# One encoder layer on one core: loads of a head's q and k apart from their rounding, first factors of w_down kept in raw buffers, weights rounded three blocks ahead

## The chip, the cores and the metric

The program runs on 1 core of one Trainium2 chip. The metric is the device time in microseconds (us) of one execution. A core has a matrix engine (PE, with its own weight loads PEld), a vector engine (DVE), a scalar engine (ACT), GpSimd (POOL), a sync engine (SP) whose work here is to issue DMAs, and 16 DMA engines that all queues share. Each engine runs its own instructions in the order written in its program; across engines they wait on semaphores.

## What is computed

Shortened from the reference, batch 1, 512 tokens, width 2048, 8 heads of 128, feed-forward width 5632, all float32:

```python
h = rms_norm(x, pre_mix_g)
z = h @ w_in                       # [q | k | v | u], 1024 columns each
a = chunked_attention(q, k, v, rel_bias)      # chunks of 64, own and 8 before
p = multiscale_pool(u, pool_w, pool_scale)    # trailing means of 2, 4, 8, 16 tokens, minus u
x = x + rms_norm(concat(a, p) @ w_o, post_mix_g)
h = rms_norm(x, pre_ffn_g)
up = causal_dwconv(h @ w_up)
y = (gelu(up[:F]) * up[F:]) @ w_down
out = x + rms_norm(y, post_ffn_g)
```

## The kernel before

**Arithmetic.** A float32 product is made of two rounded parts: `split` writes the rounded operand `hi` on ACT and the rest `lo` on DVE, and `mm3` issues three matmuls. Tile names end in `h` and `l` for these parts and in `r` for the raw load. The large projections use seven products of halves instead of eight (`mm2`, `pairs.order`), with sums and differences of weights made on DVE.

**Order.** PE's instructions stand in the order written in the program. Those of the other engines are put into each engine's queue by a scheduler that works with its own estimate of times; `tc.issue_after(x)` holds an instruction behind another. Buffers are rings by tag: `raw` has 5 tiles of 128x1024 and holds raw weights on their way in, `w4` has 8 and holds their rounded parts (4 pairs), `hT` holds the activations. A new tile of a ring waits until whatever used its place is done, a store to DRAM included.

**Weights.** `Weights` holds one list of blocks (`specs`) in order of use. `get` takes the next and loads and rounds up to `ahead` blocks beyond it. The load is issued on SP's queue, the rounding goes to ACT and DVE.

**The mixing part**, which takes the first 600 us or so, runs in these stages:

1. Head 0's q and k, straight from the input (to about 30 us); then `v_steps(0)`: the first half of v, 16 steps of 12 matmuls, while DVE, ACT and POOL make the sums and differences of the input (`x_sums`). `v_spill(0)` stores that half to DRAM (`vd`).
2. q and k of heads 1 to 7 (`qk_product`, to about 223 us), 2.8 us a product. Each head's result is stored to `zqk`. The list `more_sums` advances one step at a time: copies and adding copies of blocks of w_o and w_down from DRAM to DRAM on POOL's queue, each paced by a small instruction on DVE and POOL (`pace`).
3. `v_steps(1)`: the second half of v (blocks 4 to 7, then 0 to 3), interleaved with the attention of heads 0 to 2. `scores(h)` multiplies q with k and issues the softmax on DVE and ACT; `turn(h)` transposes the probabilities on PE and rounds them into `pth`, `ptl`; `values(h)` multiplies them with v. `load_head(h)` loads the bias and `zqk` of a head, scales (`zq` times `RR`) and rounds them (`qkh`, `qkl`); `v_load` loads v and rounds it (`vh`, `vl`). Both are called as one piece: `load_head(h + 1)` at the end of `scores(h)`.
4. `u0` to `u7` (`project`), each two weight blocks and 48 matmuls, interleaved with the attention of heads 3 to 7 and the pooling (`pool_keep`, `pool_mix`). `pool_mix` writes through one buffer `mx` and stores to `pooled`.
5. w_o (`wo_product`), from about 440 us.

Three of the first factors of w_down that are used much later (`READY`, six halves) are rounded in advance in this part and stored as rounded parts to DRAM (`rw01`, `rw11`, `rw02`, with `h` and `l`): three halves among the blocks of `v_steps(0)`, three among those of `v_steps(1)`, their parts in `w4` tiles (`keep_ready` issues the two stores).

Of the kernel before, what the change touches and what calls it, by code (L numbers as in the profile page):

```python
# [15 lines left out]
P = 128  # L16
# [63 lines left out]
def encoder_layer(ctx: ExitStack, tc: tile.TileContext, x, xT, vecs, rel, post_mix, post_ffn,  # L80
# [175 lines left out]

    READY_AT = {0: (2, 4, 6), 1: (3, 5, 7)}
    ready_parts = [(at, j) for at in READY for j in range(2)]
    READY_OF = {0: ready_parts[:3], 1: ready_parts[3:]}

    def v_and_ready_specs(g):
        specs = []
        for n, spec in enumerate(v_specs(g)):
            specs.append(spec)
            if n in READY_AT[g]:
                (cc, i), j = READY_OF[g][READY_AT[g].index(n)]
                specs.append((f"rw{cc}{i}_{j}", first_block(cc, i - 1, 0)[:, 2 * j:2 * j + 2, :], 2, 512))
        return specs

    def keep_ready(g, n):  # L270
        if n not in READY_AT[g]:
            return
        (cc, i), j = READY_OF[g][READY_AT[g].index(n)]
        for dest, v in zip(ready_w[cc, i], weights.get(f"rw{cc}{i}_{j}")):
            nc.sync.dma_start(dest[:, 2 * j:2 * j + 2, :], f32(v))
# [4 lines left out]
    for g in range(4):  # L280
        specs += u_specs(2 * g)
        if g:
            specs += pm_spec(g - 1)
        specs += u_specs(2 * g + 1)
    for i in WO:
        for cc in range(2):
            specs += wo_specs(i, cc)
        if i == 1:
            specs += pm_spec(3)
# [4 lines left out]

    weights = Weights(specs, load_w, 4)
    weights.limit = FIRST_PART
# [87 lines left out]
    def v_steps(i, ps):  # L384
        for n, c in enumerate(VORDER[i]):
            w = weights.get(f"v{i}_{c}", 2 if (i, n) == (1, 0) else None)
            if not i:
                pairs.prefetch(4 - FIRST_PART + weights.used)
            for j in range(2):
                kb = 2 * c + j  # L390
                for t in range(NT):
                    mm3(ps[t], g_tokens(hT, kb, t), part(w, j), n == j == 0, n == 7 and j == 1)
                if j:
                    keep_ready(i, n)
                    if not i:
                        pairs.prefetch(4 - FIRST_PART + weights.used)
                yield

    def v_spill(i, ps):
        for p in range(2):  # L400
            v = raw4(f"vs{p}").rearrange("p (a b) -> p a b", a=2)
            for t in range(2):
                nc.scalar.activation(v[:, t], ps[2 * p + t], AF.Copy)  # L403
            nc.sync.dma_start(vd[i][:, 2 * p:2 * p + 2, :], v)
# [35 lines left out]
    class Pairs:  # L440
# [12 lines left out]
        def load(self, k, i):  # L453
            def raw(what, tile_, m, kh):
                load_w.last = nc.sync.dma_start(tile_, w_qk[k + 1, m, kh]).ins
                self.raw[k, what] = tile_

            if i == 1:
                raw("x", p0.tile([P, 1024], F32, tag="wx", bufs=3, name="wx"), 0, 0)
                raw("w", raw4("ww"), 1, 0)  # L460
            elif i == 2:
                raw("z", raw4("wz"), 0, 1)
            elif i == 5:
                raw("y", raw4("wy"), 1, 1)

# [48 lines left out]
    psr = bank("R")  # L514
    token_sums(psr, ssum)
    rstd(rt, psr[:, :NT])
    v_spill(0, psv)

# [35 lines left out]
    def qk_keep(k, i):  # L554
# [18 lines left out]
        elif i == 4:  # L573
            one, m, a = qk_z.pop((k, "1")), qk_z.pop((k, "m")), qk_banks.pop((k, "a"))
            z = p0.tile([P, 2, S], F32, tag="z", bufs=2, name="z")
            nc.vector.tensor_add(z[:, 0, :T], one[:, 0, 0], one[:, 0, 1])
# [13 lines left out]
    for k, i in [at for at in pairs.order if at[0] is not None]:  # L590
# [24 lines left out]
    with tc.tile_pool(name="p1", bufs=2, reuse_waits="tile") as p1:  # L615
# [34 lines left out]

        def load_head(h):
            state["bias", h] = t512("bias", bufs=1)
            nc.sync.dma_start(state["bias", h], rel[h])
            nc.vector.memset(state["bias", h][:CHUNK, S - CHUNK:], -1e30)
            v = p1.tile([P, 2, S], F32, tag="zq", bufs=1, name="zq")
            nc.sync.dma_start(v, zqk[h])
            nc.vector.tensor_mul(v, v, RR)
            pair = [p1.tile([P, 2, S], F32R, tag="qk" + p, bufs=1, name="qk" + p) for p in "hl"]
            split(*pair, v)
            state["qk", h] = [tuple(p[:, n, :] for p in pair) for n in range(2)]  # L660

        def v_load(i):
            vh, vl = (acc8(f"v{p}{i}", "B", F32R).rearrange("p (a b) -> p a b", a=NT) for p in "hl")
            nc.sync.dma_start(f32(vl), vd[i])
            for t in range(NT):
                split(vh[:, t, :], vl[:, t, :], f32(vl)[:, t, :], rt[:, t:t + 1])
            state["v"] = vh, vl

        def scores(h):
            (q, k), bias = state.pop(("qk", h)), state.pop(("bias", h))  # L670
            products = [bank(f"s{h}_{t}") for t in range(1, NT)]
            products = [products[0][:, 256:], *products]
# [17 lines left out]
            if h + 1 < HEADS:  # L690
                load_head(h + 1)

# [62 lines left out]

        load_head(0)
        v_load(0)
        for h in range(3):
            run(3 if not h else 1)
            scores(h)  # L760
# [4 lines left out]
            more_sums(1)  # L765
            run(2)
            turn(h)
        run(1)
        v_spill(1, psv)

        def mid(h):
            def step():
                values(h)
                more_sums(1)
                if h == 2:
                    scores(3)
                if h == 3:
                    v_load(1)
            return step

        for j in range(8):
            ps = project(f"u{j}", mid(2 if j == 0 else j + 1) if j not in (1, 7) else None)
            if 1 <= j <= 5:
# [918 lines left out]
```

## Time and profile before

| | us |
|---|---|
| three runs: median (lowest, highest) | 1928.85 (1921.6, 1929.78) |
| the profiled execution, its time | 1925.9 |
| its span, first to last instruction | 1924.1 |
| PE busy | 1873.8 (97%) |
| DVE busy | 1541.6 (80%) |
| ACT busy | 1082.5 (56%) |
| POOL busy | 302.3 (16%) |

How to read it: the span is PE's program almost from end to end, so what can be won is where PE stands still, and where it runs at a lower granted clock. "Idle before, releaser" in a view names what ended a wait. Times in views count from the span's start. A wait for several semaphores is put down to the one that came last. Busy time of engines other than PE costs nothing by itself; it counts where PE waits for it.

### The profile page before, as it was taken

To read this page: it belongs to the slowest core of one execution; us is meant where nothing else is said; L and a number is where in the kernel's file an instruction comes from. 1 tells how busy PE (TensorE), PEld (TensorE's weight loads), DVE (VectorE), ACT (ScalarE), POOL (GpSimd) and SP (SyncE) were. 2 spreads that over 40 slices of the span, in tenths; PEclk is the share of its full clock that TensorE was granted. 3 is DMA by queue.
4 is the path that set the end of the run, shared out by engine and by line. 5 is a ranking of instruction groups with operands and counts; after the bars stand their busy time and mean duration, and the time that the engine had idled before them with its cause. 6 is when DMAs were issued, how large, how long until landed. Compare 5 with 4: busy or idle time off the path is not lost.

```text
span 1924.1 us, 25433 instructions
## 1 busy us (share of the span) xinstructions
PE 1873.8 (97%) x9598; PEld 1593.8 (83%) x9598; DVE 1541.6 (80%) x1800; ACT 1082.5 (56%) x1376; POOL 302.3 (16%) x398
## 2 busy tenths in 40 slices
PE   9999869999999999999999999999999999999998
PEld 7788757877888888888888888888888888888886
DVE  6988565867768898878888888888887799898875
ACT  8545434535646566656565656656565665565553
POOL 3211110111000022121212121222211001101101
PEclk9999979999999999999999999999999999999999
DMA  8579897789887488888888988898988977876785
GB/s 279 185 247 284 250 301 240 208 223 305 297 251 288 134 215 199 199 201 199 208 204 196 209 200 201 201 197 196 207 191 269 350 230 174 198 197 170 172 234 146
DMA packets 139770, 426.01 MB, mean 221 GB/s; under 512 B 11968, under 2 KB 15424, under 8 KB 133952
## 3 DMA queue, kind: packets, MB, share of 16 engines
q0 software_dynamic: 54864, 173.56, 44.9%
q1 hardware_dynamic: 84784, 250.84, 37.5%
q8 instruction: 75, 1.23, 0.2%
q14 instruction: 47, 0.39, 0.1%
HBM read 370.35 MB, written 104.33 MB: 247 GB/s over the span
## 4 chain that ended last, share of the span: by engine, by line
PE 86%; DVE 5%; DMA 5%; ACT 2%; issue 1%; SPq 0%; POOL 0%; DVEq 0%; POOLq 0%; ACTq 0%
PE qa L164 18%; PE qa L170 9%; PE qg L164 9%; PE qg L170 5%; PE qd L164 4%; PE pa L156 4%; PE pa L158 4%; PE pa L159 4%; PE qd L170 2%; PE m L158 2%; PE m L156 2%; PE m L159 2%; PE pg L156 2%; PE pg L158 2%; PE pg L159 2%; DMA zq<-zqk 1%
## 5 line engine op out<-in xcount | busy, mean ns | idle before, releaser
L164 PE MATMUL qa<-gT,wfh 128*128 128x512 f32 x1152 | 290.7, 394 | 4.5 <-ACT vs L403 3.5
L138 ACT ACTIVATE wfh<-wx 128x1024 fp32r<-128x1024 f32 x192 | 203.5, 1060 | 156.8 <-PE qg L164 59.2
L139 DVE TENSOR_TENSOR wfl<-wx,wfh 128x1024 fp32r<-128x1024 f32 x192 | 234.7, 1222 | 64.7 <-ACT wfh L138 47.4
L164 PEld LDWEIGHTS qa<-gT,wfh 128*128 128x128 f32 x1152 | 207.9, 189 | 42.7 <-ACT vs L403 3.7
L1319 POOL DMA_DIRECT2D wx<-in_w_up x122 | 104.6, 857 | 506.2 <-DVE wfl L139 478.0
L138 ACT ACTIVATE wfh<-wy 128x1024 fp32r<-128x1024 f32 x96 | 101.9, 1061 | 117.3 <-PE qg L164 64.1
L164 PE MATMUL qg<-h,wfh 128*128 128x512 f32 x656 | 165.7, 394 | 0.0
L170 PE MATMUL qa<-gT,wfl 128*128 128x256 f32 x1152 | 160.8, 282 | 0.0
L170 PEld LDWEIGHTS qa<-gT,wfl 128*128 128x128 f32 x1152 | 151.2, 190 | 4.6
L164 PEld LDWEIGHTS qg<-h,wfh 128*128 128x128 f32 x656 | 122.9, 188 | 28.0
L139 DVE TENSOR_TENSOR bl<-b,bh 128x2048 fp32r<-128x2048 f32 x56 | 127.3, 2286 | 22.8 <-ACT bh L138 11.7
L138 ACT ACTIVATE bh<-b 128x2048 fp32r<-128x2048 f32 x56 | 105.8, 1911 | 47.2 <-DVE b L1077 20.2
L139 DVE TENSOR_TENSOR wfl<-wy,wfh 128x1024 fp32r<-128x1024 f32 x96 | 117.2, 1221 | 16.1 <-ACT wfh L138 9.3
L156 PE MATMUL pa<-bh,ah 128*128 128x512 f32 x320 | 126.1, 394 | 0.0
L158 PE MATMUL pa<-bl,ah 128*128 128x512 f32 x320 | 125.8, 393 | 0.0
L159 PE MATMUL pa<-bh,al 128*128 128x512 f32 x320 | 125.5, 392 | 0.0
L139 DVE TENSOR_TENSOR wfl<-wz,wfh 128x1024 fp32r<-128x1024 f32 x48 | 58.7, 1223 | 54.2 <-PE qa L164 54.1
L164 PE MATMUL qd<-gT,wfh 128*128 128x512 f32 x384 | 95.7, 391 | 0.0
L170 PEld LDWEIGHTS qg<-h,wfl 128*128 128x128 f32 x656 | 89.4, 188 | 7.5
L170 PE MATMUL qg<-h,wfl 128*128 128x256 f32 x656 | 91.6, 282 | 0.0
L164 PEld LDWEIGHTS qd<-gT,wfh 128*128 128x128 f32 x384 | 72.0, 188 | 16.2
L164 PE MATMUL qa<-h,wfh 128*128 128x512 f32 x328 | 83.2, 395 | 0.0
(551 smaller groups left out, 4386.6 us busy)
## 6 DMA issues: line engine op xcount, KB each, us to landing
wx<-in_w_up POOLq DMA_DIRECT2D x122, 512.0 KB, 5.9
b<-in_w_down SPq DMA_DIRECT2D x32, 1024.0 KB, 6.7
wt<-in_w_o POOLq DMA_DIRECT2D x24, 1024.0 KB, 12.6
wx<-in_w_up SPq DMA_DIRECT2D x43, 512.0 KB, 5.4
wz<-in_w_up SPq DMA_DIRECT2D x41, 512.0 KB, 5.6
wy<-in_w_up SPq DMA_DIRECT2D x41, 512.0 KB, 4.6
wy<-in_w_up POOLq DMA_DIRECT2D x41, 512.0 KB, 6.7
sum<-part POOLq DMA_DIRECT2D x38, 512.0 KB, 5.9
```

The lines of the kernel that those rows point to most:

```text
L138: rounded = nc.scalar.activation(hi, src, AF.Copy)
L139: rest = nc.vector.tensor_sub(lo, src, f32(hi))
L156: nc.tensor.matmul(ps, l[0], r[0], start=first, stop=False, skip_group_check=onto)
L158: nc.tensor.matmul(low, l[0], r[1], start=False, stop=False, skip_group_check=onto)
L159: nc.tensor.matmul(ps, l[1], r[0], start=False, stop=last, skip_group_check=onto)
L164: nc.tensor.matmul(ps, w[0][:, kb], pairs[kb][0], start=fresh and not kb, stop=last, skip_group_check=not fresh)
L170: nc.tensor.matmul(ps[:, sl], w[1][:, kb], pair[:, sl], start=False, stop=last, skip_group_check=not fresh)
L1319: nc.gpsimd.dma_start(self.raw[k, what], self.block(k, m, kh), accum_op=ALU.add)
```

## The change

It touches the mixing part alone.

- `load_head` becomes three: `load_bias` (the load alone), `load_z` (the load of `zqk` alone) and `ready_head` (scaling, rounding, and the load of the next head's `zq` right behind). The scaling waits behind the instruction that `split` last gave to DVE (`tc.issue_after(split.rest)`). The memset in the bias moves into `scores`, ahead of its use. `ready_head(h + 1)` is called two steps of v after `scores(h)` in stage 3, and inside or behind a `project` in stage 4.
- `v_load` keeps the load, `v_ready` rounds, behind `turn(0)` (and behind `u2` for the second half).
- All six halves of `READY` move into stage 4, one behind each of `u0` to `u5`; their rounded parts lie in two of the five tiles of the ring `raw` instead of `w4`.
- `Weights` runs 3 blocks ahead, not 4, until `weights.ahead = 4` behind `u7`.
- `v_spill(0)` stands ahead of `rstd` and writes through a `z` tile (pool `p0`, 2 tiles) instead of `raw`; one `wx` and one `wy` load change places between `raw` and `p0`.
- `more_sums` takes two steps fewer in stage 2 (at product 3 of heads 6 and 7) and two more in stage 4.

```diff
     def load_w(name, src, a, b):
         n = a * b
-        raw, hi, lo = raw4(name + "r"), w4(name + "h"), w4(name + "l")
+        raw = raw4(name + "r")
+        if name[:2] == "rw":
+            hi, lo = (big.tile([P, 1024], F32R, tag="raw", bufs=5, name=name + p) for p in "hl")
+        else:
+            hi, lo = w4(name + "h"), w4(name + "l")
...
-    READY_AT = {0: (2, 4, 6), 1: (3, 5, 7)}
+    READY_AT = {0: (), 1: ()}
...
-    READY_OF = {0: ready_parts[:3], 1: ready_parts[3:]}
+    READY_OF = {0: (), 1: ready_parts}
+    READY_U = {j: j for j in range(6)}
...
-    weights = Weights(specs, load_w, 4)
+    weights = Weights(specs, load_w, 3)
...
-            v = raw4(f"vs{p}").rearrange("p (a b) -> p a b", a=2)
+            v = raw4(f"vs{p}").rearrange("p (a b) -> p a b", a=2) if i else z_tile()
...
+    v_spill(0, psv)
     rstd(rt, psr[:, :NT])
-    v_spill(0, psv)
...
-        if i in (3, 7, 4) and (k, i) != (0, 3):
+        if i in ((3, 7, 4) if 0 < k < 5 else (7, 4)):
             more_sums(1)
...
-        def load_head(h):
+        def load_bias(h):
             state["bias", h] = t512("bias", bufs=1)
             nc.sync.dma_start(state["bias", h], rel[h])
-            nc.vector.memset(state["bias", h][:CHUNK, S - CHUNK:], -1e30)
-            v = p1.tile([P, 2, S], F32, tag="zq", bufs=1, name="zq")
-            nc.sync.dma_start(v, zqk[h])
-            nc.vector.tensor_mul(v, v, RR)
+
+        def load_z(h):
+            state["z", h] = p1.tile([P, 2, S], F32, tag="zq", bufs=1, name="zq")
+            nc.sync.dma_start(state["z", h], zqk[h])
+
+        def ready_head(h):
+            v = state.pop(("z", h))
+            with tc.issue_after(split.rest):
+                nc.vector.tensor_mul(v, v, RR)
             pair = [p1.tile([P, 2, S], F32R, tag="qk" + p, bufs=1, name="qk" + p) for p in "hl"]
             split(*pair, v)
             state["qk", h] = [tuple(p[:, n, :] for p in pair) for n in range(2)]
+            if h + 1 < HEADS:
+                load_z(h + 1)
...
         def scores(h):
             (q, k), bias = state.pop(("qk", h)), state.pop(("bias", h))
+            with tc.issue_after(split.rest):
+                nc.vector.memset(bias[:CHUNK, S - CHUNK:], -1e30)
...
-        load_head(0)
+        load_z(0)
+        load_bias(0)
         v_load(0)
         for h in range(3):
-            run(3 if not h else 1)
+            if not h:
+                run(2)
+                ready_head(0)
+            run(1)
             scores(h)
             more_sums(1)
             run(1)
             if h:
                 values(h - 1)
             more_sums(1)
-            run(2)
+            run(1)
+            ready_head(h + 1)
+            run(1)
             turn(h)
+            if not h:
+                v_ready()
...
+            if j in READY_U:
+                keep_ready(1, j)
             if j < 7:
                 pool_keep(j // 2, j % 2, ps)
-                more_sums(2 if j == 6 else 1)
+                more_sums(1 + j % 2)
         u7 = ps
         more_sums.paced = False
+        weights.ahead = 4
```

PE's own instructions keep their order. On the other engines the order moves; two places matter below. The first is DVE's queue where stage 2 passes into stage 3. Before, with `v_6` and `v_7` the weight blocks of v that PE takes next, `gT` the activations that are put back, `zm` and `pth` parts of heads 7 and 0:

```order
L636 CAST pth<-tmp 128x128
L636 CAST ptl<-tmp 128x128
L654 MEMSET bias 64x64
L657 TENSOR_TENSOR zq<-zq,RR 128x1024
L142 SCALAR_TENSOR_TENSOR gT_131<-xr_2005,vec,gT_131 128x256
L139 TENSOR_TENSOR v_6l<-v_6r,v_6h 128x1024
L572 TENSOR_TENSOR zm<-zb,zm 128x512
L142 SCALAR_TENSOR_TENSOR gT_131<-xr_2005,vec,gT_131 128x256 x3
```

The same place with the change:

```order
L139 TENSOR_TENSOR v_6l<-v_6r,v_6h 128x1024
L588 TENSOR_TENSOR zm<-zb,zm 128x512
L142 SCALAR_TENSOR_TENSOR gT_131<-xr_1973,vec,gT_131 128x256 x3
L142 SCALAR_TENSOR_TENSOR gT_132<-xr_1983,vec,gT_132 128x256 x3
L139 TENSOR_TENSOR v_7l<-v_7r,v_7h 128x1024
L142 SCALAR_TENSOR_TENSOR gT_132<-xr_1983,vec,gT_132 128x256
L320 MEMSET pace 128x1
L139 TENSOR_TENSOR v_0l<-v_0r,v_0h 128x1024
L593 TENSOR_TENSOR z<-zm 128x512
L595 TENSOR_TENSOR z<-qa_1735,z 128x256
L320 MEMSET pace 128x1
L678 TENSOR_TENSOR zq<-zq,RR 128x1024
```

The memset in the bias and the scaling of head 0 stood ahead of `v_6l`; now the scaling stands behind `v_6l`, `v_7l` and `v_0l`, and the memset behind the rounding of the head.

The second is ACT's queue around the first softmax (`s,sm<-s,nm` is the exponential of one of its four tiles, `pth` the probabilities turned by PE). Before:

```order
L138 ACTIVATE v_1h<-v_1r 128x1024
L138 ACTIVATE qkh<-zq 128x1024
L685 ACTIVATE s,sm<-s,nm 128x128
L138 ACTIVATE rw_0h<-rw_0r 128x1024
L141 ACTIVATE vh_2136<-vl_2137,rt 128x512 x4
L685 ACTIVATE s,sm<-s,nm 128x256
L138 ACTIVATE v_2h<-v_2r 128x1024
L685 ACTIVATE s,sm<-s,nm 128x384
L685 ACTIVATE s,sm<-s,nm 128x512
```

With the change:

```order
L138 ACTIVATE v_1h<-v_1r 128x1024
L714 ACTIVATE s,sm<-s,nm 128x128
L714 ACTIVATE s,sm<-s,nm 128x256
L138 ACTIVATE v_2h<-v_2r 128x1024
L714 ACTIVATE s,sm<-s,nm 128x384
L138 ACTIVATE rw_0h<-rw_0r 128x1024
L714 ACTIVATE s,sm<-s,nm 128x512
L138 ACTIVATE qkh<-zq 128x1024
```

The four roundings of v and those of the next head left the middle of the softmax; one rounding of a w_down factor (`rw_0h`) still stands ahead of its last exponential.

More of the change, by code (lines that the diff above doesn't have):

```diff
@@ L265, in v_and_ready_specs @@
             if n in READY_AT[g]:
-                (cc, i), j = READY_OF[g][READY_AT[g].index(n)]
-                specs.append((f"rw{cc}{i}_{j}", first_block(cc, i - 1, 0)[:, 2 * j:2 * j + 2, :], 2, 512))
+                specs.append(ready_spec(*READY_OF[g][READY_AT[g].index(n)]))
         return specs
     def keep_ready(g, n):
-        if n not in READY_AT[g]:
+        at = READY_U if g else {m: k for k, m in enumerate(READY_AT[0])}
+        if n not in at:
             return
-        (cc, i), j = READY_OF[g][READY_AT[g].index(n)]
+        (cc, i), j = READY_OF[g][at[n]]
         for dest, v in zip(ready_w[cc, i], weights.get(f"rw{cc}{i}_{j}")):
@@ L387, in v_steps @@
             if not i:
-                pairs.prefetch(4 - FIRST_PART + weights.used)
+                pairs.prefetch(3 - FIRST_PART + weights.used)
             for j in range(2):
@@ L392, in v_steps @@
                     mm3(ps[t], g_tokens(hT, kb, t), part(w, j), n == j == 0, n == 7 and j == 1)
-                if j:
+                if j and not i:
                     keep_ready(i, n)
-                    if not i:
-                        pairs.prefetch(4 - FIRST_PART + weights.used)
+                    pairs.prefetch(3 - FIRST_PART + weights.used)
                 yield
@@ L458, in load @@
             if i == 1:
-                raw("x", p0.tile([P, 1024], F32, tag="wx", bufs=3, name="wx"), 0, 0)
+                raw("x", raw4("wx") if not k else p0.tile([P, 1024], F32, tag="wx", bufs=3, name="wx"), 0, 0)
                 raw("w", raw4("ww"), 1, 0)
@@ L463, in load @@
             elif i == 5:
-                raw("y", raw4("wy"), 1, 1)
+                raw("y", raw4("wy") if k else p0.tile([P, 1024], F32, tag="wx", bufs=3, name="wy"), 1, 1)
         def make(self, k, i):
@@ L515, in encoder_layer, with z_tile @@
     token_sums(psr, ssum)
+    def z_tile():
+        return p0.tile([P, 2, S], F32, tag="z", bufs=2, name="z")
+    v_spill(0, psv)
     rstd(rt, psr[:, :NT])
-    v_spill(0, psv)
     def spread1():
@@ L664, in v_load, with v_ready @@
             nc.sync.dma_start(f32(vl), vd[i])
+            state["v"] = vh, vl
+        def v_ready():
+            vh, vl = state["v"]
             for t in range(NT):
-                split(vh[:, t, :], vl[:, t, :], f32(vl)[:, t, :], rt[:, t:t + 1])
-            state["v"] = vh, vl
+                with tc.issue_after(split.last):
+                    split(vh[:, t, :], vl[:, t, :], f32(vl)[:, t, :], rt[:, t:t + 1])
         def scores(h):
             (q, k), bias = state.pop(("qk", h)), state.pop(("bias", h))
+            with tc.issue_after(split.rest):
+                nc.vector.memset(bias[:CHUNK, S - CHUNK:], -1e30)
             products = [bank(f"s{h}_{t}") for t in range(1, NT)]
```

17 lines of the change are left out of this document (15 added, 2 removed).

## Prediction

> **What bounds the kernel now.** I read the page's totals first, then who waited for whom on PE, then PE's, DVE's and ACT's timelines where those waits lie.
>
> ```profile
> PE 1873.8 (97%) x9598; PEld 1593.8 (83%) x9598; DVE 1541.6 (80%) x1800; ACT 1082.5 (56%) x1376; POOL 302.3 (16%) x398
> PE   9999869999999999999999999999999999999998
> PEclk9999979999999999999999999999999999999999
> ```
>
> PE sets the end. The 41 us in which it stands still lie almost wholly in slices 5 and 6 and a few places beside them, all in the mixing part. PE's own list of waits says for whom:
>
> ```profile
> PE pt L699 <- DVE s L688: 17.6, 6, 5.2
> PE v L158 <- DVE v_6l L139: 6.4, 1, 6.4
> PE s L156 <- DVE ptl L139: 3.9, 1, 3.9
> PE qa L164 <- ACT vs L403: 3.5, 1, 3.5
> PE s L158 <- DVE qkl L139: 2.5, 1, 2.5
> PE m L156 <- ACT wo_3h L138: 2.4, 1, 2.4
> PE m L158 <- DVE wo_3l L139: 1.6, 1, 1.6
> PE qa L164 <- ACT wfh L138: 1.1, 1, 1.1
> ```
>
> The first column of numbers is the total in us. After a long wait the matmuls themselves are slow; the windows show it as granted clock (PEclk), PE busy being the second number:
>
> ```profile
> 235.00:240.00 5.00, 4.13 (x10) 3.26 (x11) 5.00 (x10) 1.59 (x3) 0.00 (x0) 0.50 0.31 105
> 240.00:245.00 5.00, 2.50 (x12) 1.94 (x11) 3.55 (x7) 0.00 (x0) 1.23 (x4) 0.84 0.81 225
> 245.00:250.00 5.00, 5.00 (x18) 4.08 (x17) 1.22 (x1) 2.01 (x2) 0.00 (x0) 0.72 1.00 342
> 270.00:275.00 5.00, 4.77 (x15) 4.10 (x16) 1.20 (x2) 2.19 (x4) 0.00 (x0) 0.50 1.08 296
> 295.00:300.00 5.00, 2.55 (x7) 2.26 (x8) 4.66 (x10) 0.77 (x3) 0.00 (x0) 0.55 0.85 154
> 300.00:305.00 5.00, 5.00 (x19) 4.04 (x18) 3.47 (x12) 2.91 (x5) 1.25 (x4) 0.76 0.48 141
> 395.00:400.00 5.00, 5.00 (x19) 4.30 (x19) 4.95 (x12) 2.76 (x6) 1.57 (x4) 0.71 0.75 230
> 465.00:470.00 5.00, 4.37 (x11) 3.46 (x12) 4.20 (x5) 2.75 (x3) 1.16 (x1) 0.54 1.06 323
> ```
>
> I charge a window with its PE busy time times (1 - PEclk): 2.1 + 0.4 + 1.4 = 3.9 us from 235 to 250, 2.4 at 270, 1.1 + 1.2 = 2.3 from 295 to 305, 1.5 at 395, 2.0 at 465.
>
> **The change, part by part.** PE's instructions and their order stay, so the sum runs over its waits, in six places.
>
> A, end of the first half of v (74 to 91 us).
>
> ```profile
> 74.56 2.11 PE L164 MATMUL qa<-gT,wfh 128*128 128x512 f32 x8 [1.06 <-ACT wfh L138]
> 87.12 3.63 PE L164 MATMUL qa<-gT,wfh 128*128 128x512 f32 x8 [3.46 <-ACT vs L403]
> 86.47 1.09 ACT L403 ACTIVATE vs<-v 128x512 f32<-128x512 f32 x2 [1.66 <-DVE wy L481]
> 59.97 2.32 DVE L139 TENSOR_TENSOR rw_0l<-rw_0r,rw_0h 128x1024 fp32r<-128x1024 f32 x1
> ```
>
> PE loses 1.06 + 3.46 us and 1.5 more to the clock (3.63 against 2.11 for the same eight matmuls): 6.0. The copies `vs` of v waited for a `raw` buffer until DVE had added `wy`. With the change they go to a `z` tile and DVE has three subtractions less before this point (2.32 us the quoted one). I count 5.5 us won. Bounds: 0, if DVE stays late for another reason, to 6.0.
>
> B, first head (229 to 250 us).
>
> ```profile
> 228.17 0.11 DVE L654 MEMSET bias<- 64x64 f32 x1 [12.98 <-DMA bias<-in_rel]
> 233.06 1.23 DVE L657 TENSOR_TENSOR zq<-zq,RR 128x1024 f32<-128x1024 f32 x1 [4.78 <-DMA zq<-zqk]
> 234.60 1.22 DVE L139 TENSOR_TENSOR v_6l<-v_6r,v_6h 128x1024 fp32r<-128x1024 f32 x1
> 229.08 0.39 PE L156 MATMUL v<-v_6h,gT 128*128 128x512 f32 x1
> 235.87 0.80 PE L158 MATMUL v<-v_6l,gT 128*128 128x512 f32 x1 [6.41 <-DVE v_6l L139]
> 209.75 23.28 DMA zq<-zqk
> ```
>
> DVE stood 12.98 + 4.78 us for two loads, one of which took 23.28 us, and `v_6l`, whose rounded part had long been there, stood behind them. That is 6.41 + 2.50 + 3.9 = 12.8 us. Now `v_6l`, `v_7l` and `v_0l` stand ahead of the scaling, so the 6.41 go. What is late next is `qkl`: PE reaches the scores twelve matmuls (0.23 us from start to start) after 229.08, at 231.8. If the load still lands at 233.0, scaling, rounding and rest (1.2 + 1.06 + 1.2) end at 236.5, and 4.7 us and some 3 of clock stay: 5.0 won at the low end, 12.8 at the high. The load now has two paced copies of 1 MB and one load of 0.5 MB less ahead of it and no bias, so I take it nearer the high end: 10.8, with 2 left.
>
> C, first two turns (255 to 275, and 0.5 at 289). The 17.6 us less the 3.76 of place E are 13.8; with 2.4 of clock 16.2. DVE's softmax stood behind head 1's load, then behind four roundings of v and two of other blocks, while ACT stood for a store:
>
> ```profile
> 255.07 1.22 DVE L657 TENSOR_TENSOR zq<-zq,RR 128x1024 f32<-128x1024 f32 x1 [5.30 <-DMA zq<-zqk]
> 262.00 2.73 DVE L142 SCALAR_TENSOR_TENSOR vl<-vl,rt,vh 128x512 fp32r<-128x512 f32 x4
> 247.45 1.06 ACT L138 ACTIVATE v_0h<-v_0r 128x1024 fp32r<-128x1024 f32 x1 [10.86 <-DMA rw11h<-rw_1h]
> ```
>
> All three leave the place: `vl` is rounded behind `turn(0)`, `w4` no longer holds a tile that is being stored, and the scaling of head 1 stands behind three of the four tiles. But PE has only 36 matmuls (8.2 us) between the scores and the turn, and ACT's rounding `rw_0h` stands ahead of the last exponential, waiting for a load issued behind the 1 MB load of v. I leave 5 us: 11.2 won. Bounds: 3, if that load takes the 20.2 us that `v_1r` took here (its row stands below), to 16.2.
>
> D, third head (297 to 303): 3.86 + 2.3 = 6.2. DVE's `ptl` stood behind two u roundings that waited for stores from `w4`. Won 4.2; 0 to 6.2, because DVE has the same work in less time.
>
> E, stage of u (310 to 440).
>
> ```profile
> 391.18 0.11 DVE L654 MEMSET bias<- 64x64 f32 x1 [4.75 <-DMA bias<-in_rel]
> 393.50 0.98 PE L699 MATMUL pt<-ident,s 128*128 128x128 f32 x7 [3.76 <-DVE s L688]
> 368.69 0.69 ACT L749 ACTIVATE mx<-pm,vec 128x512 f32<-128x512 f32 x1 [4.85 <-DMA pooled<-mx]
> 310.00:440.00 130.00, 125.69 (x614) 106.38 (x614) 89.86 (x217) 58.86 (x115) 13.07 (x25) 0.99 0.81 232
> ```
>
> The memset of the next head's bias stood in the middle of a softmax; now it opens its own softmax. 3.76 + 1.5 = 5.2, of which 4 won. Against it come six roundings: six times 1.06 us of ACT and 1.22 of DVE, 7.3 on DVE's 89.9 of 130. That still leaves a quarter of DVE free, but each stands in a queue ahead of something, and `mx`, which holds the exponentials behind it for a store, will hold them longer on busier DMA engines. I charge 5 us; bounds 0 to 20 (the six roundings in full, with the clock after each turn: six times 2.3 + 1.0).
>
> F, start of w_o (463 to 470).
>
> ```profile
> 462.14 1.06 ACT L138 ACTIVATE wo_3h<-wo_3r 128x1024 fp32r<-128x1024 f32 x1 [10.46 <-DMA wo_3r<-in_w_o]
> 440.00:500.00 60.00, 55.74 (x234) 44.91 (x233) 50.19 (x57) 36.64 (x44) 5.08 (x8) 0.94 1.03 301
> ```
>
> 2.42 + 1.58 + 2.0 = 6.0 us, by a load on DMA engines that are full already (share 1.03). Nothing here gets better; what the stage before leaves behind arrives here. I charge 3, bounds 0 to 12 (twice what stands there now).
>
> Three blocks ahead instead of four:
>
> ```profile
> u_0r<-in_w_u SPq DMA_DIRECT2D x6, 512.0 KB, 7.2
> v_1r<-in_w_v SPq DMA_DIRECT2D x1, 512.0 KB, 20.2
> ```
>
> The last column is us from issue to landing. A block of v or u covers 24 matmuls (5.5 us), so three cover 16 us: enough for the 7.2 us of a load in the stage of u, and nothing in my sum. At the 20.2 us of the full stretch around 220 us, each block would come 4 us late.
>
> Sum: 5.5 + 10.8 + 11.2 + 4.2 + 4 - 5 - 3 = 27.7 us, against the profiled execution's own 1925.9 us (1924.1 span and 1.8 around it), so **1898 us**. That execution lies 3 us under the median of the runs shown, inside their range.
>
> [...]
>
> **The rivals.**
>
> *The waits move.* The late loads of `zq`, `vl` and `rw_0r` are late because the DMA engines are full, and that stays. For it speaks the 23.28 us of a 0.5 MB load; against it that three w_down halves and two copies leave this stretch. Then B wins 5.0 and C 3, A 5.5, D 2, E and F together lose 4: 11.5 won, 1914 us.
>
> *The DMA engines become the bound from 310 us on.* Six halves bring 1.5 MB each, with two paced copies 11.5 MB into a stage that moves 232 GB/s: 50 us of transfers, where a share of 0.81 leaves 25 us of 130 free. It decides once that free share can't be used, because SP's queue stands in order behind stores into `raw` and `pooled`. With A to D won in full (31.7) and all 50 lost, E and F unchanged: 1944 us. For it speak F's share over 1.0; against it that a good part of POOL's copies is wanted only hundreds of us later.
>
> [...]
>
> *DVE or ACT holds each turn in the stage of u:* charge 20, not 5, and F 6: 1916 us.
>
> **How the numbers follow.** Chances: forecast 0.56 (own range 1884 to 1911), waits move 0.22, DMA bound 0.12, DVE or ACT bound 0.10. A measurement of this kernel can tell 0.5%, 9.6 us, from no change, so faster is under 1919: all of the first, 0.16 of the second, 0.05 of the fourth, 0.77. Same: 0.05 + 0.02 + 0.04 = 0.11, with 0.02 of the third. Slower: 0.10 of the third and 0.02 of the rest, 0.12. The range runs from 1882 (F charged nothing, B and C near their best) to 1923 (the second and fourth cases with a little more lost in F).
>
> **What would show it.** In the new profile PE's waits for `v_6l` and for `vs` are gone, DVE's longest wait for a load around 220 to 240 us is for `zq` alone and shorter than 12.98 us, the turns' 17.6 falls under 8, and no PE wait stands behind a store of `rw`. Wrong it is if PE's wait at the first scores or turn is over 8 us (loads still late), if new waits for `u_0h`, `u_1l` or `wo` parts add more than 10 us, or if the clock falls where there was no wait.

## The result, and the profile after

The changed kernel takes 1922.2 us (median of 20 runs, 1918.9 to 1925.5), the kernel before 1925.1 us (20 runs): a ratio of 0.9987, 95% interval 0.998 to 0.9994. The forecast was 1898 us. The gain that the prediction saw ahead of `u0`, 31.7 us, was made to 30.3 us, and nearly all of it was lost again behind: the table shows it by marks that both traces have.

| from | to | before, us | after, us | difference | forecast |
|---|---|---|---|---|---|
| start | second half of v | 212.6 | 206.2 | -6.4 | -5.5 (A) |
| second half of v | first matmul of u0 | 99.6 | 75.7 | -23.9 | -26.2 (B, C, D) |
| u0 | u7 (last block of u) | 118.0 | 136.0 | +18.0 | +1 (E) |
| u7 | first matmul of w_o (`m`) | 10.9 | 12.4 | +1.5 | 0 |
| `m` | first matmul of w_up | 165.9 | 174.2 | +8.3 | +3 (F) |
| first of w_up | end | 1317.1 | 1317.7 | +0.6 | 0 |

The marks are rows of PE's timeline. Of the kernel after, u0, u7, `m` and w_up (first number: start in us):

```profile
281.91 0.47 PE L160 MATMUL u<-gT,u_0h 128*128 128x512 f32 x1
417.95 0.39 PE L160 MATMUL u<-gT,u_0h 128*128 128x512 f32 x1
430.30 0.50 PE L160 MATMUL m<-wo_0h,a 128*128 128x512 f32 x1 [1.29 <-ACT a L138]
604.46 0.36 PE L160 MATMUL up<-gT,w_0h 128*128 128x256 f32 x1
```

The same four of the kernel before:

```profile
312.21 0.48 PE L156 MATMUL u<-gT,u_0h 128*128 128x512 f32 x1
430.19 0.39 PE L156 MATMUL u<-gT,u_0h 128*128 128x512 f32 x1
441.08 0.39 PE L156 MATMUL m<-wo_0h,a 128*128 128x512 f32 x1
606.98 0.36 PE L156 MATMUL up<-gT,w_0h 128*128 128x256 f32 x1
```

At u0 the new kernel is 30.3 us ahead, at u7 12.2, at w_up 2.5. Who PE waits for now, from the list of waits of the kernel after (total, times, longest):

```profile
PE pt L728 <- DVE s L717: 20.8, 7, 10.4
PE m L160 <- ACT wo_3h L138: 7.6, 1, 7.6
PE u L160 <- DVE ptl L139: 2.3, 1, 2.3
PE pt L728 <- DVE pace L320: 2.0, 2, 1.1
```

The waits for `v_6l`, `vs` and `qkl` are gone. The turns' wait is larger than the 17.6 us of before, and lies elsewhere: once at the first head and, but for 0.4 us, for the rest at the turns of the stage of u. PE's busy slices tell where: what stood in slices 5 and 6 now stands in 6, 8 and 10 (240 to 480 us):

```profile
PE   9999989798999999999999999999999999999998
PEclk9999989898999999999999999999999999999999
```

PE's timeline from 320 to 420 us, the rows with a wait:

```profile
325.28 0.98 PE L728 MATMUL pt<-ident,s 128*128 128x128 f32 x7 [0.91 <-DVE pace L320]
333.32 0.80 PE L160 MATMUL u<-gT,u_0h 128*128 128x512 f32 x1 [2.34 <-DVE ptl L139]
349.13 0.30 PE L728 MATMUL pt<-ident,s 128*128 128x128 f32 x1 [1.11 <-DVE tmp L757]
351.04 0.47 PE L728 MATMUL pt<-ident,s 128*128 128x128 f32 x1 [1.61 <-DVE s L717]
352.65 0.48 PE L728 MATMUL pt<-ident,s 128*128 128x128 f32 x1 [1.14 <-DVE pace L320]
355.40 1.76 PE L728 MATMUL pt<-ident,s 128*128 128x128 f32 x7 [2.27 <-DVE s L717]
376.25 0.33 PE L728 MATMUL pt<-ident,s 128*128 128x128 f32 x1 [2.42 <-DVE s L717]
379.61 1.76 PE L728 MATMUL pt<-ident,s 128*128 128x128 f32 x7 [3.02 <-DVE s L717]
```

That is 14.8 us of waits; with 0.7 at 401 us it is 15.5. The windows add the slow clock behind them (PE busy, then granted clock after POOL's column):

```profile
330.00:360.00 30.00, 21.53 (x86) 17.32 (x85) 19.12 (x45) 13.45 (x28) 2.73 (x4) 0.78 0.85 230
360.00:385.00 25.00, 19.56 (x86) 16.60 (x86) 16.79 (x43) 9.21 (x19) 2.94 (x6) 0.85 0.89 240
```

21.53 x 0.22 + 19.56 x 0.15 = 7.7 us. Together 23.2, against the 5.2 that the prediction charged here before and a wait of 0.6 at 360 us: most of the 18 us of the table.

Behind them stand loads. ACT's and SP's timelines of the kernel after, from 322 to 358 us:

```profile
323.45 0.38 SPq L687 DMA_DIRECT2D vl<-vd  x1
326.39 0.33 SPq L154 DMA_DIRECT2D u_0r<-in_w_u  x1
329.09 0.47 SPq L284 DMA_DIRECT2D rw11l<-rw_1l  x1
329.60 1.24 SPq L154 DMA_DIRECT2D rw_0r<-in_w_down  x1
...
347.92 0.33 SPq L284 DMA_DIRECT2D rw02h<-rw_0h  x1
...
357.48 0.42 SPq L154 DMA_DIRECT2D u_0r<-in_w_u  x1
```

```profile
346.83 1.06 ACT L138 ACTIVATE rw_0h<-rw_0r 128x1024 fp32r<-128x1024 f32 x1 [9.97 <-DMA rw_0r<-in_w_down]
347.80 0.38 ACT L714 ACTIVATE s<-s,nm 128x128 f32<-128x128 f32 x1
```

The half `rw_0r`, issued at 329.6 as the last of a bunch, lands 17.2 us later. ACT stands 9.97 us for it, with the exponentials of a softmax behind it in its queue, and SP stands at the store of the half until 347.9, with the next loads of u behind it.

### The profile page after: what moved, and what is told of

Same layout as the page of the kernel before. It is cut to its first block, busy times and chain, and to the rows that moved or that the text cites. A ratio compares the mean times of both kernels' runs of the same rounds, so it can differ in the third digit from the quotient of the medians.

```text
span 1922.2 us, 25415 instructions
## 1 busy us (share of the span) xinstructions
PE 1873.5 (97%) x9598; PEld 1593.1 (83%) x9598; DVE 1540.0 (80%) x1800; ACT 1082.9 (56%) x1376; POOL 301.5 (16%) x398
## 4 chain that ended last, share of the span: by engine, by line
PE 88%; DMA 6%; DVE 3%; ACT 2%; issue 1%; SPq 0%; DVEq 0%; POOL 0%; POOLq 0%; ACTq 0%
PE qa L168 18%; PE qa L174 10%; PE qg L168 9%; PE qg L174 5%; PE qd L168 5%; PE pa L160 4%; PE pa L162 4%; PE pa L163 4%; PE qd L174 2%; DMA rw_0r<-in_w_down 2%; PE m L163 2%; PE m L162 2%; PE m L160 2%; PE pg L160 2%; PE pg L162 2%; PE pg L163 2%
## 5 line engine op out<-in xcount | busy, mean ns | idle before, releaser
L168 PEld LDWEIGHTS qd<-gT,wfh 128*128 128x128 f32 x384 | 72.0, 188 | 16.2
```

The lines of the kernel that those rows point to most:

```text
L168: nc.tensor.matmul(ps, w[0][:, kb], pairs[kb][0], start=fresh and not kb, stop=last, skip_group_check=not fresh)
```

## The experiments

All start from the changed kernel; e2, e3 and e19 leave out the rounding of the six factors. A table gives the marks of each profiled run; below stands each edit. A ratio is to runs of the kernel before made alongside, whose medians lie between 1923.6 and 1926.6 us. The stretches come from one profiled execution of each kernel, so differences of one or two us between them tell nothing: e7, which changes only the start of w_o, reaches u0 1.8 us earlier than the kernel after.

| run | u0 at, us | u0 to u7 | `m` to w_up | median, us | ratio to before (95%) |
|---|---|---|---|---|---|
| before | 312.2 | 118.0 | 165.9 | 1925.1 | |
| after | 281.9 | 136.0 | 174.2 | 1922.2 | 0.9987 (0.998 to 0.9994) |
| e1 halves back in v | 297.3 | 117.1 | 172.7 | 1920.9 | 0.9979 (0.997 to 0.9988) |
| e2 no halves | 300.1 | 116.9 | 171.2 | 1919.2 | 0.9959 (0.9946 to 0.9972) |
| e3 no rounding | 275.7 | 131.4 | 174.1 | 1910.0 | 0.9921 (0.9906 to 0.9936) |
| e4 rounding late | 276.3 | 133.6 | 171.0 | 1920.8 | 0.9981 (0.9971 to 0.999) |
| e5 four ahead | 281.3 | 136.7 | 171.9 | 1920.1 | 0.9962 (0.9949 to 0.9975) |
| e6 two sum steps back | 288.4 | 131.7 | 168.0 | 1918.1 | 0.9952 (0.9937 to 0.9968) |
| e7 `mixT` behind `wo_3r` | 280.1 | 135.6 | 168.1 | 1915.3 | 0.994 (0.9921 to 0.996) |
| e8 stores by POOL | 284.8 | 141.5 | 172.8 | 1926.6 | 1.0002 (0.999 to 1.0014) |
| e10 halves in w_o, e7 | 276.9 | 118.6 | 195.0 | 1918.9 | 0.9968 (0.9956 to 0.9981) |
| e11 sums of w_down out | 281.6 | 134.5 | 164.7 | 1911.7 | 0.9939 (0.992 to 0.9958) |
| e12 e11 and e7 | 282.2 | 135.3 | 163.8 | 1910.8 | 0.9931 (0.9917 to 0.9945) |
| e14 halves in w4 | 276.6 | 134.7 | 173.7 | 1914.0 | 0.9947 (0.9928 to 0.9966) |
| e15 w4, rounding late | 277.3 | 147.4 | 169.6 | 1931.9 | 1.004 (1.0026 to 1.0054) |
| e16 e15, stores by POOL | 276.2 | 154.0 | 169.2 | 1930.6 | 1.0034 (1.0021 to 1.0048) |
| e17 e15, e11, e7 | 278.8 | 143.8 | 168.9 | 1916.0 | 0.9958 (0.9943 to 0.9972) |
| e18 POOL rounds | 277.6 | 140.7 | 170.1 | 1914.6 | 0.9938 (0.9922 to 0.9953) |
| e19 rounding, no transfer | 278.9 | 117.3 | 170.6 | 1908.3 | 0.9914 (0.989 to 0.9937) |
| e20 e14, sums out from step 24 | 276.1 | 115.0 | 186.5 | 1908.8 | 0.9915 (0.9902 to 0.9929) |

### Where the gain came from, and what the halves cost: e1 and e2

```diff
-    READY_AT = {0: (), 1: ()}
-    READY_U = {j: j for j in range(6)}
+    READY_AT = {0: (2, 4, 6), 1: (3, 5, 7)}     # e1, hi and lo from w4
+    READY_U = {}
```

> The six halves go back among the blocks of v, in the w4 buffers; the split of load and rounding, the z tiles and three blocks ahead stay. Marks on PE in the changed kernel: second half of v begins at 206.2 us, u0 at 281.9, u7's second weight half at 418.0, the first matmul of w_up at 619.2. Theory 'place' (the halves cost what they cost where ACT's queue has their rounding in front of exponentials) and theory 'traffic' (their bytes on DMA engines that are full) both expect u0 to u7 back from 136.0 us to about 118, the length before the change. What it tells apart is the gain of the first three heads: if it came from taking the halves out of this stretch, u0 begins near 305 us; if from rounding behind the softmax instead of ahead of it, near 285, and the kernel ends near 1908.

u0 begins at 297.3 us, between the two numbers expected, but 6.0 us of that are a new wait for `v_7l` in the first half of v, whose second half begins at 214.1 us: with the halves back, and three blocks ahead, the gain of A is gone too. From the second half of v to u0 it takes 83.1 us, against 99.6 before and 75.7 after. So the new places of the scaling and rounding give 16.5 us and the halves' leaving 7.4 more. The stage of u is back at 117.1: its 19 us are the halves'.

```diff
-    READY_U = {j: j for j in range(6)}
+    READY_U = {}
+    for cc, i in READY:                # behind the stage of w_o
+        for dest in ready_w[cc, i]:
+            nc.gpsimd.dma_start(dest, first_block(cc, i - 1, 0))
```

> No half of w_down is loaded, rounded or stored in the mixing part; the later stage's tensors get a plain copy of w_down once the stage of w_o is over, so the output is computed with unrounded words. Both theories, place and traffic: u0 to u7 falls from 136.0 us to 118 or less, u7's second weight half is reached by 400 us. If instead it stays above 130, neither is right: then three blocks ahead, or the two sums that moved into this stage, made it longer. If the stage of w_o is bound by its own loads, w_up begins less than 18 us earlier than 619.2: near 610; if it only passes on what the stage before left, near 601.

The scheduler put the plain copies, which wait for nothing, at the program's start, where they delayed everything by some 23 us (the second half of v begins at 229.7). The stretches behind that still tell: u0 to u7 is 116.9. `m` to w_up stays at 171.2 without any half, so at most 3 of F's 8.3 us are theirs.

### The stage of u: rounding work, queues, buffers

```diff
-        split(hi[:, :n], lo[:, :n], raw[:, :n])
+        if name[:2] == "rw":
+            return tuple(raw[:, :n].rearrange("p (a b) -> p a b", a=a) for v in (hi, lo))   # e3
+            return hi, lo, raw                          # e4, with the split in keep_ready
+        split(hi[:, :n], lo[:, :n], raw[:, :n])
```

> The halves are loaded and the raw words stored twice, with no rounding on ACT and no subtraction on DVE (the output then lacks the rounding of these factors); bytes and DMAs are those of the changed kernel. Theory place expects u0 to u7 near 120 us and the end near 1907; theory traffic expects it unchanged, 132 to 138 us, end 1918 to 1924.

> The halves are loaded as early as in the changed kernel, but rounded where they are stored, a block of u later, when the load has long landed. Bytes and instructions are those of the changed kernel. Theory place: ACT no longer waits for rw_0r and rw_1r (15 us in 280 to 460 us), u0 to u7 near 124 us, end near 1912. Theory traffic: u0 to u7 132 to 138 us, end 1918 to 1924, and the waits move to u_0h and mx.

e3 falls between the theories: 131.4 us, of which 15.2 are one wait. ACT stood 20.0 us for `vl`, the second half of v: SP issued that load only at 323.9, having stood 8.6 us for a raw buffer that a half's store was still reading, and it took 10.5 us. The rest of the stage takes 116.2. e4 gives back 2.4 us of 19: ACT stands 3.5 us for the halves' loads, not 15, but then for `u_0r` (11.6 us), for the store under `mx` (22.8, the last one behind the stage, where PE's 10 us for `a` follow) and for buffers. So the place of the rounding alone is not the cause.

```diff
+        weights.ahead = 4                               # e5, ahead of v_spill(1)
-            nc.sync.dma_start(dest[:, 2 * j:2 * j + 2, :], f32(v))
+            nc.gpsimd.dma_start(dest[:, 2 * j:2 * j + 2, :], f32(v))    # e8
-            hi, lo = (big.tile([P, 1024], F32R, tag="raw", bufs=5, name=name + p) for p in "hl")
+            hi, lo = w4(name + "h"), w4(name + "l")     # e14
```

> Weights are again rounded four blocks ahead from the end of v on; the halves stay in the stage of u. Marks in the changed kernel: u0 281.9, u7 417.9 us (136.0 apart; 118.0 before the change and 117 with the halves taken out). Theory 'three ahead is too few' expects u0 to u7 to fall to 120 to 126 us, since ACT's waits for u_0r (23.7 us in all) go. Theory traffic expects 132 to 138: with the five raw buffers shared with the halves, a load four blocks ahead waits for a buffer instead.

> The stores of the rounded halves are issued by POOL's queue, not SP's. Theory 'SP stands': SP's 59 us behind rw stores go, the loads of u behind them are issued earlier, u0 to u7 near 125, end near 1912. Theory traffic: the loads are issued earlier and land as late; 133 to 138, end within 3 us of 1922.

> The rounded halves lie in w4 buffers, so a half takes one raw buffer, not three; all else as in the changed kernel. Theory 'raw buffers': loads behind a half are no longer held, u0 to u7 falls from 136.0 us to 118 to 124. Theory 'ACT's queue': ACT still stands for rw_0r, 130 to 137. Theory traffic: 133 to 138.

None of them gives the time back: 136.7, 141.5 and 134.7 us. Three blocks ahead did cost nothing. Storing by POOL is worse; why is not shown. SP no longer stands at the halves' stores there, but POOL stands up to 20.8 us for a rounding ahead of a store, with its copies behind it. e14 wins 5.3 us ahead of u0: the half's rounding no longer stands ahead of the last exponential of the first softmax, and the first turn's wait falls from 10.4 to 5.6 us.

```diff
+        raw, pair = weights.get(f"rw{cc}{i}_{j}"), [w4(f"rw{p}") for p in "hl"]   # e15, in keep_ready
+        split(*pair, raw)                               # e16: and its stores by nc.gpsimd, as in e8
```

> As e14, and the halves are rounded where they are stored, a block after their load. Theory 'several queues, each enough': u0 to u7 117 to 122 here where e4 (133.6) and e14 alone are longer. Theory 'raw buffers': as e14. Theory 'SP's queue' (the stores wait for a rounding that is now later): 128 to 136. Theory traffic: 133 to 138.

> As e15, with the stores issued by POOL's queue. Theory 'SP's queue': u0 to u7 117 to 120 and shorter than e15 by 5 us or more. Theory 'raw buffers' and 'several queues': within 3 us of e15. Theory traffic: 133 to 138.

All the theories fail: 147.4 and 154.0, longer than all others. Taken late, the w4 tiles stand in the ring between those of u, and ACT's `u_0h` waits for the half's stores (`rw01h`, `rw11h`, `rw02h`: 34 us in e15).

```diff
+        if name[:2] == "rw":                            # e18
+            nc.gpsimd.tensor_copy(hi[:, :n], raw[:, :n])
+            nc.gpsimd.tensor_sub(lo[:, :n], raw[:, :n], f32(hi[:, :n]))
+            split(hi, lo, RR)                           # e19, no load and no store
```

> POOL, busy 1 us in 8 in this stage, makes the rounded half and the rest; loads, stores and buffers are those of the changed kernel. Theory 'work in the chain of the softmax': u0 to u7 falls from 136.0 us to 117 to 122, end near 1905. Theory traffic or buffers: 133 to 138; longer, if POOL takes so long that the buffers are held.

> Six roundings at the same places, of a tile that is always there (RR): no load and no store of the halves (the later stage's tensors get a plain copy of w_down after the stage of w_o, so its words are unrounded). Theory 'work in the chain of the softmax': u0 to u7 stays at 128 to 136 us. Theory 'loads and stores' (traffic, buffers or queues): 117 to 121.

With e3, these two settle the work. With all six roundings on ACT and DVE and no transfer the stage takes 117.3 us; with the transfers and none of that work on ACT and DVE it takes 131.4 (e3) and 140.7 (e18, where POOL, which also issues the copies, does it). (In e19 the plain copies behind w_o cost 12 us after the first matmul of w_up, so its whole time says less than this stretch.)

### The stage of u: the transfers

```diff
-                more_sums(1 + j % 2)
+                more_sums(2 if j == 6 else 1)                        # e6
-        if i in ((3, 7, 4) if 0 < k < 5 else (7, 4)):
+        if i in (3, 7, 4) and (k, i) != (0, 3):
+            if more_sums.n < more_sums.most:                         # e11: most = 32 until u7
+                next(sums_step, None)
+    more_sums.n, more_sums.most = 0, 24                              # e20, with e14's w4
```

> The two steps of paced copies and adds (2 MB in DRAM) that moved into the stage of u go back ahead of 220 us; the halves stay. Theory traffic, if every byte counts alike: about a fifth of the 19 us (2 MB against the 9.4 MB of the halves), so u0 to u7 near 132 and u0 no earlier than 281.9, rather later. If the sums are what fills the stage, 125 or less. If neither, 136 and u0 later.

> The halves stay in the stage of u as in the changed kernel; what leaves it are the paced copies and adds of w_down's sums (t, 1 MB each, seven of them from 377 to 417 us), which go to the stage of w_o. ACT, DVE and SP keep their work and order in the stage of u. Theory traffic: the second half of the stage gets its time back: u4 (360.6) to u7 (417.9), 57.3 us now and 54 to 51 without halves (e2: 48.3, before the change 53.8), falls to about 50, and u0 to u7 to 128; loads of u land in under 8 us there. Theory place (ACT's queue order): unchanged, 134 to 138, 57 for u4 to u7. The start of w_o: without t copies at 405 to 475 us wo_3r lands sooner, first m to w_up 165 to 170 unless the copies cost the same later.

> e14 (rounded halves in w4) with the sums held at the 24th step until u7, so that no more copy or add into wt is issued in the stage of u from about its start on; the 24 steps left go to the stage of w_o, two behind each product's start. Theory traffic (the DMA engines can't carry the halves and the copies at once): the halves' loads land in 4 to 8 us and u0 to u7 falls from 134.7 us (e14) to 118 to 123. Theory 'SP's order alone': 130 to 136, since SP's and ACT's order is that of e14. First m to w_up: 164 as in e11 if the stage of w_o has room for 8 MB more, else 170 to 185; the end 1895 to 1900 by theory traffic with room there.

e6 gives back 4.3 us, the fifth that theory traffic expected, and loses 6.5 ahead of u0. e11 misses: u4 to u7 takes 56.1 us. It took away the copies that begin at 377 us (one comes back at 396.8, issued by SP), and the stalls above lie from 325 to 380, while POOL's adds into `wt` run. The DMA view of the changed kernel, 320 to 340 us (KB each, us from issue to landing):

```profile
wt<-in_w_o POOLq DMA_DIRECT2D x1, 1024.0 KB, 19.5
u_1r<-in_w_u SPq DMA_DIRECT2D x1, 512.0 KB, 10.7
rw11l<-rw_1l SPq DMA_DIRECT2D x1, 512.0 KB, 15.9
rw_0r<-in_w_down SPq DMA_DIRECT2D x1, 512.0 KB, 17.2
```

e20 holds these too (no copy or add is issued from 265 to 373 us), and the whole cost is gone with all six halves in place: 115.0 us, PE's waits in the stage 2.3 us, against 13.8 in e14. Landing times of the halves' loads, 285 to 400 us, of e14, which still has the copies, and then of e20:

```profile
rw_0r<-in_w_down SPq DMA_DIRECT2D x2, 512.0 KB, 11.4
rw_1r<-in_w_down SPq DMA_DIRECT2D x2, 512.0 KB, 7.0
```

```profile
rw_0r<-in_w_down SPq DMA_DIRECT2D x2, 512.0 KB, 6.2
rw_1r<-in_w_down SPq DMA_DIRECT2D x2, 512.0 KB, 5.0
```

So the stage takes 117 us with the copies and no halves' transfers (e2, e19), 115 with the halves and no copies (e20), and 135 with both (e14). Little else differs between e14 and e20: SP's order in the stage is the same but for one load of a bias, ACT's but for a few instructions, most of them behind 345 us, and the small paced instructions that leave with the copies take DVE 0.06 to 0.08 us each, with no wait ahead of them. The windows of e14 and then of e20 show it at 320 to 360 us (the last three numbers are clock, DMA share, GB/s):

```profile
320.00:340.00 20.00, 17.54 (x76) 15.28 (x77) 12.30 (x26) 6.58 (x12) 0.00 (x0) 0.83 1.05 337
340.00:360.00 20.00, 14.96 (x61) 12.35 (x60) 17.61 (x48) 11.75 (x27) 2.73 (x4) 0.83 0.79 191
```

```profile
320.00:340.00 20.00, 18.52 (x91) 15.16 (x89) 18.07 (x40) 14.01 (x28) 0.00 (x0) 1.00 0.66 217
340.00:360.00 20.00, 19.36 (x99) 16.61 (x100) 17.43 (x40) 9.02 (x19) 0.00 (x0) 1.00 0.56 184
```

The 24 steps that left come back in the stage of w_o: `m` to w_up 186.5 us, against 164.7 with 16 of them there (e11). e20 still ends 14.9 us under the kernel before. For that the end that was expected, 1895 to 1900, is not reached. Among the versions that leave nothing out its median is the lowest; the intervals of e11 and e12 overlap with its own.

### The start of w_o: e7, e10, e11, e12, e17

In the kernel after, the load `wo_3r`, for which PE waits 7.6 us, stands on SP behind a load of `pooled`, which waits for its own store:

```profile
429.32 0.34 SPq L779 DMA_DIRECT2D pooled<-mx  x1
443.81 0.34 SPq L842 DMA_DIRECT2D mixT<-pooled  x1
444.24 0.39 SPq L154 DMA_DIRECT2D wo_3r<-in_w_o  x1
```

```diff
-        ps1 = [wo_product(1, cc, a11) for cc in range(2)]
+        ps1 = [wo_product(1, 0, a11)]
+            with tc.issue_after(load_w.last):           # e7: moved here, behind wo_3r
+                nc.sync.dma_start(mixT[n][:, sl, :], pooled[:, 4 * (n - 2) + sl.start:4 * (n - 2) + sl.stop, :])
+        ps1.append(wo_product(1, 1, a11))
+            if (i, cc) in READY_WO:                     # e10: a half behind six of the products
+                specs.append(ready_spec(*READY_OF[1][READY_WO[i, cc]]))
```

> Only SP's order at the start of w_o changes: the two loads mixT<-pooled stand behind wo_3r instead of in front of it. Theory 'F is SP's queue': wo_3r no longer waits for the store of pooled (14.0 us), is issued by 432 us, and PE's wait of 7.6 us for wo_3h with its slow clock is gone; first m to first w_up falls from 174.2 to about 165, the end comes near 1913. Theory 'F is full DMA engines': wo_3r lands as late as before, the wait stays over 5 us.

> The six halves are loaded, rounded and stored in the stage of w_o, behind products at about 500 to 580 us, where DMA share is 0.69 to 0.96 and ACT and DVE are busy half the time; the mixT loads stand behind wo_3r as in e7. Against e7 only the halves' place differs (e7: u0 280.1, u7 415.7, m 426.6, w_up 594.7, span 1911.4). Theory traffic, and theory place too: u0 to u7 falls from 135.6 to 117. Traffic: they cost something where they go, since the engines are 0.7 to 1.0 busy there too, but the loads of w_o are issued 11 us ahead of their use: first m to w_up 168 to 176; the end 1894 to 1902. Theory place alone: no cost there, 168, end 1893.

> e11 and e7 together: sums of w_down in the stage of w_o, mixT loads behind wo_3r, halves in the stage of u. If the start of w_o suffers from both SP's order and full engines, PE's wait there (7.6 us in the changed kernel, 6.2 in e7) falls under 2 us, first m to w_up near 160, end near 1900; if the copies cost the same later, m to w_up stays at 166 to 170 and the end at 1905 to 1910.

> e15 with the sums of w_down in the stage of w_o (e11) and the mixT loads behind wo_3r (e7). If the halves cost nothing in e15, m is reached near 410 us; first m to w_up 164 to 172 as in e11 and e12; end 1893 to 1900. Theory traffic: m at 428, end near 1910 as e12.

e7: `wo_3r` is issued at 427.9, its wait goes, and 6.1 of the 8.3 us come back; a wait of 6.2 us for `wo_1h` takes its place. The load `wo_1r` has landed by then (11.3 us after 415.74), but ACT, which rounds it next, stands for the load of `mixT` that was moved back and takes 16.2 us beside POOL's copies of `t`:

```profile
444.61 1.06 ACT L138 ACTIVATE a<-mixT 128x1024 fp32r<-128x1024 f32 x1 [11.44 <-DMA mixT<-pooled]
```

e11, which takes most of the copies away, has no such wait there and gains 9.5; e12 adds 0.9, which is within the spread. So F has two causes, and removing either gives most of it back. e10 shows that the halves' price moves with them: the stage of u is at 118.6, but w_o takes 27 us more than in e7 (195.0, where at most 176 was expected), since the half's stores stand on SP ahead of `wo_0r` (PE waits 9.1 us for `wo_0h` in one place). e17 carries e15's loss.

## Why the prediction was wrong

**A to D came near their sum, but not term by term.** They are worth 30.3 us by the marks, 31.7 in the sum. By its own charges (waits, and PE busy times the missing clock) A, B and D won all they could, 6.0, 12.8 and 6.2, together 4.5 us more than forecast: PE has no wait there and the clock is 1.00 from 295 to 305 us. C won 3.3 of 11.2, near its lower bound. One cause is the one that the bound named: a rounding of a half ahead of the last exponential, with a load of 18.7 us. Rows of PE, of ACT and of the windows:

```profile
246.37 1.75 PE L728 MATMUL pt<-ident,s 128*128 128x128 f32 x7 [10.35 <-DVE s L717]
243.84 1.06 ACT L138 ACTIVATE rw_0h<-rw_0r 128x1024 fp32r<-128x1024 f32 x1 [12.07 <-DMA rw_0r<-in_w_down]
```

```profile
235.00:250.00 15.00, 4.65 (x19) 3.82 (x18) 5.30 (x8) 4.79 (x8) 0.00 (x0) 0.70 0.64 231
250.00:275.00 25.00, 24.57 (x123) 20.83 (x122) 21.37 (x51) 12.68 (x27) 5.41 (x8) 0.97 0.85 175
295.00:305.00 10.00, 10.00 (x46) 8.28 (x45) 9.05 (x19) 5.00 (x11) 0.00 (x0) 1.00 0.94 338
```

10.35 and 0.43 us of waits (at 246 and 265 us) and 4.65 x 0.30 + 24.57 x 0.03 = 2.1 of clock are left of 16.2. All charges sum to 28.3; the other 2 us were not traced. That C's miss of 7.9, the 4.5 and these 2 nearly cancel is luck.

The half's rounding is about half of the first turn's 10.35 us. Where none stands ahead of that exponential, the turn still waits 5.1 (e3) to 7.4 us (e19). DVE then stands for the load of head 1's `zq`: its scaling was put behind three of the four tiles, and so ahead of the fourth, which PE's turn needs too. Rows of DVE in e10, where PE waits 5.70 us:

```profile
239.64 1.23 DVE L681 TENSOR_TENSOR zq<-zq,RR 128x1024 f32<-128x1024 f32 x1 [6.43 <-DMA zq<-zqk]
240.98 0.48 DVE L720 TENSOR_SCALAR s<-s,rs 128x512 f32<-128x512 f32 x1
```

So the scaling alone uses up the 5 us that the prediction left there for the few matmuls ahead of the turn and the half's rounding together.

**E is the step that failed**: "I charge 5 us" for six roundings, with 4 won. It charged the work of the roundings and a store that holds `mx` longer. The work by itself costs nothing (e19, 117.3 us), and the price, 19 us, is that of 9.4 MB of loads and stores beside POOL's copies (e14 against e20): the loads land late, and ACT and SP stand for them in order. Nor did the 4 us show that were to be won: without the halves the stage takes 116.9 to 117.4 us (e1, e2, e19), against 118.0 before. The rival "the DMA engines become the bound from 310 us on" had the mechanism, with a chance of 0.12, and put its price at 50 us, of which 18 came. (The 31.7 us that it calls won in full are the forecast of A to D; in full, by the charges, they would be 41.2.) SP's queue in order was also in that rival's text; the runs add that late loads cost where an engine in order stands on them, and that moving one such stand (e4, e8, e14, e15) only brings the next to the front.

The rival "DVE or ACT holds each turn" gave 1916 us, nearest to the result. The turns of the stage of u do wait for DVE and ACT, but these stand for loads; that the roundings themselves hold them, as its charge of 20 us has it, e19 excludes. The range's lower end, 1882, does not follow from the terms named for it: with F at nothing and B and C at 12.8 and 16.2 the sum gives 1888.

**F** was charged 3 and cost 8.3 (and 1.5 ahead of it), inside its bounds. "What the stage before leaves behind arrives here" was right for the copies (e11, 164.7 us against 174.2); that SP stands 14 us behind a store ahead of the load was not seen, though the trace of before has the same place: there the store of 437.68 us lets the load go at 445.92, 8.2 us later.

**Three blocks ahead** cost nothing, as said (e5, with four: 136.7 us against 136.0).

**What would show it.** `v_6l` and `vs` are gone from PE's waits, and DVE's longest wait for a load from 220 to 247 us is for `zq`, 5.75 us: right. The turns' wait, to fall under 8, is 20.8: wrong, and PE's wait at the first turn, 10.35, is over the 8 us that the prediction set as the sign of loads that are still late.

With POOL's copies gone, the halves' loads on SP land in 5.0 and 6.2 us (e20), not 7.0 and 11.4 (e14). How the DMA engines share their time among the queues, no run here shows.

## What to carry to other kernels

Before moving transfers into a stage, add the bytes that other queues move there at that time, not over the whole stage: background copies that are wanted only later are the first thing to move, and here they were worth more in the stage (19.7 us, e14 to e20) than any reordering of the work that waits (2.4 us, e4). A load in front of which several engines stand in order was hardly mended one queue at a time (e4, e8, e14, e15: 133.6 to 147.4 us, against 136.0); measure the work without the transfers and the transfers without the work before anything else. A change that brings a stage forward gains only what the next stage's loads can follow, here 2.5 us at w_up out of 30.3 at u0: look at what SP stands behind at the seam.

## What the hardware showed that was not expected

Transfers issued by POOL, here copies and adds from DRAM to DRAM, took more of the DMA engines' time per MB than those issued by SP, most of them loads. The queues of the kernel after from 405 to 475 us (packets, MB, share of 16 engines):

```profile
q0 software_dynamic: 3774, 10.48, 68.0%
q1 hardware_dynamic: 3387, 8.88, 35.9%
```

That is 6.5% of the time per MB against 4.0. Whether the adds, the way from DRAM to DRAM or the queue makes the difference is not shown.

The granted clock also fell after several short waits: none of those from 349 to 353 us in the rows above is longer than 1.61 us, and the single transpose goes from 0.30 us to 0.47. PE is busy 1.1 us of the 4 from 349 to 353 us, and the granted clock goes from 1.00 (347 to 349 us) to 0.50 (351 to 353 us).
